# A two-layer hybrid decoder step on one core: rounding of operands moved to ScalarE, sums over values in two halves of one bank, a summed product in the state mixer, and a written-out order in the last output projection

## The chip, the cores and the metric

One Trainium2 chip, one core of it. The metric is the device time of one launch in microseconds (us). The kernel before took 1351.92 us (median of three runs, 1343.92 to 1352.94). The execution that the profiler recorded took 1348.51 us; its span, from the first to the last instruction, is 1346.5 us.

## What is computed

One inference step of two layers for a prompt of 1024 tokens and for 8 samples of 4 new tokens each, 1056 rows of 1024 features in all. Cut to what matters:

```
layer 0: h = rmsnorm(x);  xa, ga, q, k, v, gb = split(h @ w_in_ab)
         ya = RG-LRU(conv4(xa)) * silu(ga)                     # mixer A
         yb = dilated window attention(q, k, v) * silu(gb)     # mixer B, 8 heads of 64
         x  = x + concat(ya, yb) @ w_out_ab
layer 1: h = rmsnorm(x);  qc, kc, vc, gc, qd, fd, idd, gd = split(h @ w_in_cd)
         yc = rmsnorm(differential attention(qc, kc, vc)) * silu(gc)   # mixer C, 4 heads
         yd = rmsnorm(HGRN2(qd, fd, idd)) * silu(gd)                   # mixer D, 4 heads, state 128x128
         x  = x + concat(yc, yd) @ w_out_cd
y = rmsnorm(x)
sample rows attend to 256 cached keys and values (C: gathered by page table) and continue the states
```

In D a sample row's output has a part from the state that it starts with: for sample b, head j and token t it is the product of the decayed query of t with S0[b] (128x128).

## The kernel before, in words

Features lie on partitions and tokens run along the free dimension. A product that must be exact to nearly fp32 is made of rounded operands: a value is split in a high part (rounded to the replicated-fp32 type that TensorE reads in one pass) and a low part (value minus high part), and three matmuls (high by high, low by high, high by low) sum in one bank. A plain fp32 matmul shows as two records in the trace. PSUM has eight banks of 512 fp32 columns here: two for projections (`pj`), three for scores (`sc`), two for transposes (`tp`), one for sums over values (`pv`).

Six stages follow one another. The instruction names in the trace begin with the stage's letter.

- **n, a** (0 to 145 us): the norm of the input, its turn to feature rows, mixer A.
- **b** (145 to 462): mixer B, the first attention. `attention` (L1824 on) projects v, q and k for each of four pairs of heads (`qkv`), scores query blocks of 128 against keys (`scores`), and sums over values by groups of 256 queries (`groups_b`). For a group, `pv_transpose` (L701) turns the probabilities, ScalarE makes the high part PH (L704), VectorE the low part PL (L705), and L736 multiplies both by the values into one `pv` bank. At a group's end ScalarE copies the upper 64 partitions of the bank (L741) and VectorE adds the lower ones into Y (L742). VectorE rounds values (L496), queries (L520) and two copies of keys (L542, L543); GpSimd makes the low parts of keys and values (L497, L544, L545), and in this stage also those of the weights (L384).
- **o** (462 to 600): the output projection of layer 0 (`out_proj`), nine row tiles of 16 steps, each step three matmuls of 512 columns (L1201 to L1203). The attention of the sample rows (`sample_attn`) is a generator that is advanced inside these steps: transposes of cached keys (L926), logits (L936, L939), softmax (L941 to L948), the turn of the probabilities (L951, L952), products with cached values (L981, L982 cast them; L1003), a gather of the rows (L1009 to L1011).
- **d** (600 to 915): mixer D. `mixer_d` yields for each head the times from which its next step can run, `weave_d` places projection steps between. At a head's end, L1473 and L1475 add the sample part: one matmul for the new tokens, then for each of 8 samples one with S0[b] as the stationary operand and 4 columns moving. L1486 updates the states. `norm_d` follows (L1237 to L1253).
- **c** (915 to 1204): mixer C, the second attention, in the manner of b; `pv` sums at L788 and L790, copied at L794.
- **p** (1204 to 1346): the output projection of layer 1 with the sample rows of mixer C. Its cached keys and values come by indirect transfers that GpSimd issues (L1998), into five buffers in turn.

The order of work: in b, c and d a planner (`weave`, `weave_d`) writes out TensorE's order (`manual_schedule`), by clocks that it keeps for each engine with fixed costs (`spend`); `pv_free` is the planned time at which the `pv` bank is read out, and a group's first product over values isn't placed ahead of it. The other engines' order, and TensorE's in o and p, is set by the framework when the kernel is built, from its own model of times. On each engine the instructions then run in that order, each waiting for its semaphores. The framework also places all semaphore waits, from the tiles that instructions touch. `steps` in `out_proj` is the generator of the sample rows; six of each eight steps advance it by one, in the first five row tiles; what is left runs ahead of tile 5. Row tile 8 holds the sample rows and comes before the last tile.

The operands of row tile 0 of an output projection are prepared ahead, after the fifth of eight weight tiles (`finish_layer`, `operands`): the half that comes from mixer A or D at once, the other half (`rest`, with its load of `yb`) at the tile's start.

Of the kernel before, what the change touches and what calls it, by code (L numbers as in the profile page):

```python
# [8 lines left out]
F32 = mybir.dt.float32  # L9
# [40 lines left out]
def _constants():  # L50
# [19 lines left out]
    blk = blk.reshape(3 * NS, NB)  # L70
    psel = np.zeros((2, P, 4, 16), f)
    for r in range(P):
# [12 lines left out]
        "c_perm": np.ascontiguousarray(np.eye(P, dtype=f).reshape(32, 4, P)[:, ::-1].reshape(P, P)), "c_blk": blk, "c_psel": psel.reshape(2, P, 64), "c_csel": csel, "c_row": np.arange(P, dtype=np.int32)[:, None].copy(),  # L85
# [10 lines left out]
class Trunk:  # L96
# [255 lines left out]
    def to_xt(self, xn, rows, t0, pools=None):  # L352
        nc = self.nc
        for half in range(2):
            pt = self.tpsum() if pools is None or half == 0 else self.T(self.ps_s, [P, 512], F32, "sc")
# [6 lines left out]
            nc.vector.tensor_tensor(lo, src, hi.bitcast(F32), ALU.subtract)  # L362

# [35 lines left out]

    def project(self, *jobs):  # L400
        for _ in self.projection(*jobs):
            pass

    def projection(self, *jobs):
# [7 lines left out]
        for t0, n in BLKS:  # L412
            for (hi, lo), (_, _, evac) in zip(ws, jobs):
                ps = self.pj()
                xh_, xl_ = self.xt(t0, n)
                for k in range(KC):
                    xh, xl = xh_[:, k], xl_[:, k]
                    nc.tensor.matmul(ps[:, :n], hi[:, k], xh, start=(k == 0), stop=False)  # L418
                    nc.tensor.matmul(ps[:, :n], lo[:, k], xh, start=False, stop=False)  # L419
                    nc.tensor.matmul(ps[:, :n], hi[:, k], xl, start=False, stop=(k == KC - 1))  # L420
# [61 lines left out]
    def qkv(self, w, cols, outs, j, split):  # L482
# [30 lines left out]
        def split_q(a, t0, t1):  # L513
# [6 lines left out]
            nc.vector.tensor_copy(hi, src)  # L520
            nc.vector.tensor_tensor(lo, src, hi.bitcast(F32), ALU.subtract)
            self.spend("dve", 0.2 + (t1 - t0) * 1.8e-3, self.clk["act"])
# [13 lines left out]
        def split_k(a, t0, t1):  # L536
# [5 lines left out]
            nc.vector.tensor_copy(Kh[a][s, t0:t1], src)  # L542
# [3 lines left out]
            t = self.spend("dve", 0.3 + (t1 - t0) * 1.2e-3, self.clk["act"])  # L546
# [163 lines left out]

    def groups_b(self, j):

        nc, T = self.nc, self.T
        for a in range(2):
            bt = [None]
            for qc in (QLB if j == 3 and (a or QB) else QCS):
# [22 lines left out]
                def end(qc, a=a, acc=acc):  # L739
                    tmp = T(self.ap_, [64, 256], F32, "pvt")  # L740
                    nc.scalar.copy(tmp, acc[0][64:128, :256])  # L741
                    nc.vector.tensor_tensor(self.Y[64 * a:64 * a + 64, j % 2, 256 * qc:256 * qc + 256], acc[0][0:64, :256], tmp, ALU.add)  # L742
# [4 lines left out]
    def groups_c(self, h):  # L747
# [8 lines left out]
        for qc in (QLC if h == 3 else QCS):  # L756
# [27 lines left out]
            def mm(kb, p, low, q0, first, last, acc=acc):  # L784
                if first:
                    acc.append(T(self.ps_v, [P, 512], F32, "pv"))
# [6 lines left out]
            def end(qc, acc=acc):  # L793
                nc.scalar.copy(self.Y[:, h % 2, 256 * qc:256 * qc + 256], acc[0][:, :256])  # L794
# [4 lines left out]
    def weave(self, groups, after, fill, pace):  # L799
# [12 lines left out]
        more, through, prog, pv_free = True, -1, 0.0, 0.0  # L812
        inf = float("inf")
        while parts or tv:
# [12 lines left out]
            if tv and (not parts or parts[0][0] > tv[0][0]):  # L827
# [3 lines left out]
                else:  # L831
                    t_at = max(held[i, kp][1], pv_free) + LAG[2]
# [4 lines left out]
            if t_at <= max(pe, s_at):  # L837
# [12 lines left out]
                if kp == qc:  # L850
                    pv_free = end(qc)
# [12 lines left out]
    def sample_attn(self, m, load_k, load_v, is_c):  # L864
# [50 lines left out]
        for g in range(2):  # L915
            sc = T(self.ps_s, [P, 512], F32, "sc")
            for b4 in range(4):
# [4 lines left out]
                for jj in range(2):  # L922
# [6 lines left out]
                    yield  # L929
# [7 lines left out]
            yield  # L937
# [10 lines left out]
            nc.vector.tensor_scalar(pr, pr, st[:, 4:5], None, ALU.mult)  # L948
            pt = self.tpsum()
# [22 lines left out]
            yield  # L972
        psel = sc1[:, :64].rearrange("p (j c) -> p j c", j=4)
        nc.sync.dma_start(psel, self.I["c_psel"][m].rearrange("p (j c) -> p j c", j=4))
# [12 lines left out]
        for g in range(2):  # L987
            banks = [T(self.ps_s, [P, 512], F32, "sc") for _ in range(4 // per)]
# [4 lines left out]
            yield  # L993
            for b4 in range(4):
# [5 lines left out]
                for hf in range(2):  # L1000
# [4 lines left out]
                    yield  # L1005
            out = T(self.ps_v, [P, 512], F32, "pv")
            ev = T(self.wp, [P, 2, 512], F32, "wraw")
            for q, ob in enumerate(banks):
# [3 lines left out]
                yield  # L1012
# [1082 lines left out]
```

## Time and profile before

| what | value |
|---|---|
| three runs, median (lowest, highest) | 1351.92 us (1343.92, 1352.94) |
| the profiled execution: time, span | 1348.51 us, 1346.5 us |
| mean granted TensorE clock | 0.98 of 2.4 GHz |
| busy: PE, VectorE, ScalarE, GpSimd | 1289.3, 820.2, 598.2, 320.3 us |
| TensorE weight loads | 1162.3 us |
| moved by DMA | 118.9 MB, mean 88 GB/s |

PE is TensorE's matmuls, PEld its weight loads, DVE VectorE, ACT ScalarE, POOL GpSimd, SP the engine that issues most DMAs. A busy PE isn't PE at its peak: matmuls overlap, so what a stretch costs is read from the distance of starts. A bracket at the end of a timeline row says how long the engine was idle before it and what ended the wait. The granted clock is a share of 2.4 GHz; 0.5 is its lower level of 1.2 GHz. L12 is line 12 of the kernel before.

### The profile page before, as it was taken

The page shows a single profiled execution, that of the slowest core. Times are in us where ns is not written, and L with a number is a line of the kernel's source. Part 1 is how long each engine was busy: PE and PEld are TensorE (multiplying, and loading weights), DVE is VectorE, ACT ScalarE, POOL GpSimd, SP SyncE. Part 2 cuts the span into 40 slices and gives each one's busy share as a digit, 9 for nine tenths or more (in the row PEclk, how much of TensorE's full clock was granted, in tenths as well). Part 3 has the DMA queues.
Part 4 walks back from the last instruction along what each step waited for, and adds up shares of the span by engine and source line. Part 5 has one row for each costly group of instructions (what it writes and reads, how often), then busy time and mean ns, then how long its engine had stood idle before and what let it go on. Part 6 is the DMA issues. An engine that isn't in the chain of part 4 may idle for free. (4 is left out here: it accounts for less than half of the span.)

```text
span 1346.5 us, 21366 instructions
## 1 busy us (share of the span) xinstructions
PE 1289.3 (96%) x8329; PEld 1162.3 (86%) x8329; DVE 820.2 (61%) x1842; ACT 598.2 (44%) x1193; POOL 320.3 (24%) x316
## 2 busy tenths in 40 slices
PE   9999999999999889999999999999999999988997
PEld 7998999989898767879999999999898888776785
DVE  7665678787877746453646465631666566674644
ACT  7466454545455535332141414132555455563522
POOL 3456844333321300001010101012212111054300
PEclk9999999999999899999989899999999999999999
DMA  7111421312131465342111112123221223145532
GB/s 218 51 60 48 129 58 41 96 47 80 34 109 33 157 214 162 98 127 83 32 50 33 49 33 65 34 96 97 65 79 49 79 64 111 47 168 183 165 120 70
DMA packets 123674, 118.90 MB, mean 88 GB/s; under 512 B 8687, under 2 KB 104857, under 8 KB 123566
## 3 DMA queue, kind: packets, MB, share of 16 engines
q1 hardware_dynamic: 102148, 96.18, 23.1%
q10 hardware_dynamic: 18866, 12.98, 3.1%
q0 software_dynamic: 2560, 8.39, 1.9%
q8 instruction: 65, 1.06, 0.3%
q14 instruction: 35, 0.29, 0.1%
HBM read 89.20 MB, written 28.33 MB: 87 GB/s over the span
## 5 line engine op out<-in xcount | busy, mean ns | idle before, releaser
L418 PE MATMUL dpj<-oXh,dwhi 128*128 128x256 f32 (+2 forms) x384 | 134.1, 349 | 1.2 <-ACT dff L1273 1.2
L418 PE MATMUL cpj<-oXh,cwhi 128*128 128x256 f32 (+2 forms) x384 | 132.7, 346 | 0.5 <-ACT ct L593 0.5
L418 PE MATMUL bpj<-Xh,bwhi 128*128 128x256 f32 (+2 forms) x384 | 127.9, 333 | 0.4 <-ACT bt L525 0.4
L420 PE MATMUL dpj<-oXl,dwhi 128*128 128x256 f32 (+2 forms) x384 | 127.4, 332 | 0.0
L419 PE MATMUL dpj<-oXh,dwlo 128*128 128x256 f32 (+2 forms) x384 | 127.4, 332 | 0.0
L420 PE MATMUL cpj<-oXl,cwhi 128*128 128x256 f32 (+2 forms) x384 | 124.6, 324 | 0.0
L419 PE MATMUL cpj<-oXh,cwlo 128*128 128x256 f32 (+2 forms) x384 | 124.4, 324 | 0.0
L420 PE MATMUL bpj<-Xl,bwhi 128*128 128x256 f32 (+2 forms) x384 | 124.2, 324 | 0.0
L419 PE MATMUL bpj<-Xh,bwlo 128*128 128x256 f32 (+2 forms) x384 | 124.1, 323 | 0.0
L384 POOL TENSOR_TENSOR cwlo<-cwraw,cwhi 128x1024 fp32r<-128x1024 f32 x16 | 38.5, 2403 | 223.0 <-ACT cwhi L382 215.5
L418 PEld LDWEIGHTS cpj<-oXh,cwhi 128*128 128x128 f32 x384 | 72.8, 190 | 12.7 <-issue 9.2
L418 PEld LDWEIGHTS dpj<-oXh,dwhi 128*128 128x128 f32 x384 | 75.2, 196 | 3.1 <-ACT dff L1273 1.5
L419 PEld LDWEIGHTS dpj<-oXh,dwlo 128*128 128x128 f32 x384 | 75.4, 196 | 0.7
L420 PEld LDWEIGHTS dpj<-oXl,dwhi 128*128 128x128 f32 x384 | 75.2, 196 | 0.3
L418 PEld LDWEIGHTS bpj<-Xh,bwhi 128*128 128x128 f32 x384 | 72.6, 189 | 2.0 <-ACT bt L525 0.8
L635 ACT ACTIVATE bP<-bP,bsst 128x128 f32<-128x128 f32 (+3 forms) x64 | 49.6, 776 | 55.6 <-DVE bsst L632 37.9
L419 PEld LDWEIGHTS cpj<-oXh,cwlo 128*128 128x128 f32 x384 | 73.0, 190 | 1.0 <-issue 0.7
L419 PEld LDWEIGHTS bpj<-Xh,bwlo 128*128 128x128 f32 x384 | 72.8, 190 | 1.1 <-issue 0.2
L420 PEld LDWEIGHTS cpj<-oXl,cwhi 128*128 128x128 f32 x384 | 72.8, 190 | 0.3
L420 PEld LDWEIGHTS bpj<-Xl,bwhi 128*128 128x128 f32 x384 | 72.5, 189 | 0.2
L705 DVE TENSOR_TENSOR bPL<-btp,bPH 128x512 fp32r<-128x512 f32 (+1 forms) x80 | 49.2, 631 | 12.3 <-ACT bPH L704 11.6
L1201 PE MATMUL opj<-oohi,owhi 128*128 128x512 f32 x128 | 51.6, 403 | 2.1 <-ACT owhi L1149 2.1
(528 smaller groups left out, 3449.0 us busy)
## 6 DMA issues: line engine op xcount, KB each, us to landing
bwraw<-in_w_in_ab_dram SPq DMA_DIRECT2D x16, 512.0 KB
dwraw<-in_w_in_cd_dram SPq DMA_DIRECT2D x16, 512.0 KB
cwraw<-in_w_in_cd_dram SPq DMA_DIRECT2D x16, 512.0 KB
nx<-in_x_prompt_dram SPq DMA_DIRECT2D x8, 512.0 KB
bBT<-aline SPq DMA_DIRECT2D x8, 512.0 KB
owraw<-in_w_out_ab_dram SPq DMA_DIRECT2D x8, 512.0 KB
owraw<-in_cache_win_k_dram SPq DMA_DIRECT2D x8, 512.0 KB
oxres<-in_x_prompt_dram SPq DMA_DIRECT2D x8, 512.0 KB
```

The costliest lines, as they stand in the source:

```text
L384: (nc.vector if self.ph == "d" else nc.gpsimd).tensor_tensor(lo, raw, hi.bitcast(F32), ALU.subtract)
L418: nc.tensor.matmul(ps[:, :n], hi[:, k], xh, start=(k == 0), stop=False)
L419: nc.tensor.matmul(ps[:, :n], lo[:, k], xh, start=False, stop=False)
L420: nc.tensor.matmul(ps[:, :n], hi[:, k], xl, start=False, stop=(k == KC - 1))
L635: nc.scalar.activation(pr[:, :nk], pr[:, :nk], AF.Exp, bias=st[:, 2:3], accum_out=st[:, 3:4])
L705: nc.vector.tensor_tensor(pl[:, :w], pt[:, :w], ph[:, :w].bitcast(F32), ALU.subtract)
L1201: nc.tensor.matmul(ps[:rows], yh[:, kk, :rows], whi[:, c], start=(k == 0), stop=False)
```

## The change

Five things. (1) In the first attention ScalarE instead of VectorE rounds the high part of queries and of one of the two copies of keys; in both attentions it rounds the high part of values. The planner's costs follow. (2) In both attentions the sums over values use one `pv` bank that is allocated once, its two halves of 256 columns by turns, and the planner lets a group begin when the group before the last has been read out. (3) In mixer D the sample part is made in two moves: 8 matmuls with the 32 sample queries as the stationary operand and S0[b] moving (128 columns), four samples in four groups of 32 output partitions of one `sc` bank and two groups of them side by side; a copy to SBUF by ScalarE; then two matmuls with that copy as the stationary operand and a constant (`own`) of zeros and ones that picks each row's own sample. (4) The generator of the sample rows is cut in pieces in another order (keys of both groups before the first turn of probabilities) and yields how many steps to leave free; in the last output projection each of the 16 steps of a tile is a slot for it that honours these numbers, and TensorE's order there is the program's. In the output projection of layer 0 the numbers are ignored and the order stays the framework's. (5) The load of `yb` for row tile 0 is issued ahead of the split of the first half. `products` and the list that `to_xt` returns only regroup code.

```diff
@@ qkv, keep: values, both attentions
-                nc.vector.tensor_copy(hi, s[:, :, x])
+                nc.scalar.copy(hi, s[:, :, x])
                 nc.gpsimd.tensor_tensor(lo, s[:, :, x], hi.bitcast(F32), ALU.subtract)
-            t = self.spend("dve", 0.2 + 0.2 * split)
+            t = self.spend("act", 0.2 + 0.3 * split)
@@ split_q
-            nc.vector.tensor_copy(hi, src)
+            nc.scalar.copy(hi, src)
             nc.vector.tensor_tensor(lo, src, hi.bitcast(F32), ALU.subtract)
@@ split_k
-            nc.vector.tensor_copy(Kh[a][s, t0:t1], src)
+            nc.scalar.copy(Kh[a][s, t0:t1], src)
             nc.vector.tensor_copy(Kh[a][o, t0:t1], src)
@@ sums over values
+    def half_bank(self):
+        self.npv += 1
+        return self.pvb[:, 256 * (self.npv % 2):256 * (self.npv % 2) + 256]
...
-                        acc.append(T(self.ps_v, [P, 512], F32, "pv"))
+                        acc.append(self.half_bank())
...
-                    t_at = max(held[i, kp][1], pv_free) + LAG[2]
+                    t_at = max(held[i, kp][1], pv_free[0]) + LAG[2]
...
-                    pv_free = end(qc)
+                    pv_free = [pv_free[1], end(qc)]
@@ sample_attn, the new order
+        yield 10
+        yield from keys(0)
+        yield 2
+        logits(0)
+        yield 1
+        yield from keys(1)
+        yield 2
+        turned(0)
+        yield 0
+        logits(1)
+        nc.sync.dma_start(psel, self.I["c_psel"][m].rearrange("p (j c) -> p j c", j=4))
+        yield 2
+        banks = []
+        yield from values(0, banks)
+        turned(1)
+        yield 2
+        yield from ends(0, banks)
+        yield 1
+        banks = []
+        yield from values(1, banks)
+        yield 3
+        yield from ends(1, banks)
@@ operands, row tile 0
+        there = second() if i == 0 else None
         split(o, src)
...
@@ out_proj
+        def slot():
+            nonlocal hold
+            if not spaced:
+                return next(steps, None)
+            if hold:
+                hold -= 1
+            else:
+                hold = next(steps, 0)
...
-                    if k % 4 and i < 5:
-                        next(steps, None)
+                    if spaced or k % 4 and i < 5:
+                        slot()
@@ mixer_d
-        yield self.pv_free
+        yield self.scq[0]
+        ps = T(self.ps_s, [P, 512], F32, "sc")
+        for b in range(NB):
+            s0 = NS * (b % 4)
+            nc.tensor.matmul(ps[s0:s0 + NS, P * (b // 4):P * (b // 4) + P], qa[:, SEQ:NT], S0[:, b], start=True, stop=True)
+        E = T(pool, [P, 2, P], F32, "E")
+        nc.scalar.copy(E.rearrange("p r v -> p (r v)"), ps[:, :2 * P])
+        e_at = self.spend("act", 0.35, self.spend("pe", 0.55) + 0.1)
+        self.sc_done(e_at)
+        yield max(self.pv_free, e_at + 0.8)
         acc = T(self.ps_v, [P, 512], F32, "pv")
         nc.tensor.matmul(acc[:, :NS], V[:NS, 8], atS, start=True, stop=False, skip_group_check=True)
-        for b in range(NB):
-            nc.tensor.matmul(acc[:, TS * b:TS * b + TS], S0[:, b], qa[:, SEQ + TS * b:SEQ + TS * b + TS], start=False, stop=(b == NB - 1),
-                             skip_group_check=True)
+        for r in range(2):
+            nc.tensor.matmul(acc[:, :NS], E[:, r], self.own[:, r], start=False, stop=(r == 1), skip_group_check=True)
@@ finish_layer
-            self.out_proj(op, o2, ws, halves, resid, done, steps, new_xt, first)
+            if self.ph == "o":
+                return self.out_proj(op, o2, ws, halves, resid, done, steps, new_xt, first, False)
+            with self.tc.manual_schedule(engines={mybir.EngineType.PE}):
+                self.out_proj(op, o2, ws, halves, resid, done, steps, new_xt, first, True)
@@ attention
+            self.npv, self.pvb = 0, T(self.ps_v, [P, 512], F32, "pv")
@@ phase_d
+            self.own = T(self.tp_, [P, 2, NS], F32, "own")
+            nc.sync.dma_start(self.own, I["c_own"].rearrange("p (r t) -> p r t", r=2))
```

## Rows read from the trace of the kernel before

**Rows 1.** Busy time by stage: b, o, d, c, p; after the engines clock, DMA.
```profile
170.00:462.00 292.00, 276.76 (x1818) 264.31 (x1816) 232.06 (x597) 153.48 (x324) 92.05 (x74) 0.98 0.22 69
462.00:600.00 138.00, 131.23 (x682) 101.59 (x681) 73.31 (x171) 54.23 (x119) 6.42 (x20) 0.98 0.49 155
600.00:915.00 315.00, 307.66 (x2397) 295.30 (x2397) 161.62 (x283) 87.52 (x151) 32.88 (x24) 0.97 0.20 58
915.00:1204.00 289.00, 282.46 (x1848) 251.84 (x1847) 174.87 (x463) 151.48 (x316) 57.99 (x35) 0.99 0.24 73
1204.00:1346.50 142.50, 125.59 (x623) 97.30 (x621) 72.07 (x175) 52.84 (x120) 34.18 (x50) 0.96 0.46 148
```

**Rows 2.** Waits of PE, longest in total: us, times, longest.
```profile
PE bpv L736 <- DVE bY L742: 6.4, 5, 1.8
PE ptp L926 <- DMA pXh<-in_cache_k_c_dram,cidx: 4.7, 3, 2.2
PE ptp L951 <- issue: 4.6, 1, 4.6
...
PE otp L926 <- DMA owraw<-in_cache_win_k_dram: 2.9, 1, 2.9
```

**Rows 3.** Timeline of PE in d, first head, and a window behind it.
```profile
689.07 2.02 PE L1475 MATMUL dpv<-dqa,dS 128*128 128x4 f32 x16
690.94 1.20 PE L1486 MATMUL dsc<-dvx,dk 96*128 96x512 f32 x2
...
691.80:695.20 3.40, 3.40 (x14) 3.30 (x14) 3.40 (x5) 0.64 (x1) 2.64 (x2) 0.64 0.80 230
```

**Rows 4.** Chain of waits and PE timeline in p: start, us.
```profile
1247.65 1.86 PE psc L936 x30
...
1227.50 0.97 PE L939 MATMUL psc<-acs,pXh 128*128 128x32 f32 x8
```

**Rows 5.** VectorE's busy time in 140 to 465 us: L542, L520, L496.
```profile
140.00:465.00 325.00, 15.62 (x20) 0.98 0.25 77
...
140.00:465.00 325.00, 10.09 (x20) 0.98 0.25 77
...
140.00:465.00 325.00, 10.06 (x16) 0.98 0.25 77
```

**Rows 6.** One line's instructions: count, ns lowest/median/highest.
```profile
L981 ACT CAST pXl<-pXh x16: 603/622/627, 1233.3 to 1273.9; 128x512 fp32r<-128x512 f32 x16
```

**Rows 7.** Timeline in b where VectorE and GpSimd read SBUF together.
```profile
177.15 0.50 PE L624 MATMUL bsc<-bKh,bQ 128*128 128x512 f32 x1 [1.30 <-DVE bsst L627]
...
366.61 2.40 POOL L384 TENSOR_TENSOR bwlo<-bwraw,bwhi 128x1024 fp32r<-128x1024 f32 x1
366.77 2.53 DVE L542 CAST bKh<-bt 64x512 fp32r<-64x512 f32 x1
...
371.17 0.41 PE L736 MATMUL bpv<-bPH,bV 128*128 128x256 f32 x2 [0.87 <-DVE bY L742]
```

**Rows 8.** Timeline in b around the longest wait for the bank.
```profile
286.77 1.07 ACT L704 CAST bPH<-btp 128x512 fp32r<-128x512 f32 x2
...
287.40 1.28 DVE L705 TENSOR_TENSOR bPL<-btp,bPH 128x512 fp32r<-128x512 f32 x2
287.62 0.47 PE L736 MATMUL bpv<-bPH,bV 128*128 128x256 f32 x2 [1.77 <-DVE bY L742]
```

**Rows 9.** Timeline in p: VectorE reads 256 columns of a bank.
```profile
1228.51 0.43 DVE L941 CUSTOM_DVE_ANT_0 pXh<-psc,pXh 128x256 f32<-128x256 f32 x1 [3.22 <-PE psc L939]
```

**Rows 10.** Timeline in p around the longest wait, and the window behind.
```profile
1233.29 1.27 ACT L981 CAST pXl<-pXh 128x512 fp32r<-128x512 f32 x2 [8.48 <-DMA pXh<-in_cache_v_c_dram,cidx]
...
1237.25 0.66 PE L951 MATMUL ptp<-pXh 128*128 128x128 f32 x2 [4.57 <-issue]
...
1237.80:1241.20 3.40, 3.40 (x14) 2.91 (x13) 1.56 (x13) 3.02 (x12) 0.00 (x0) 0.62 0.45 121
```

**Rows 11.** Timeline of ACT in p: the eighth weight tile.
```profile
1211.22 1.05 ACT L1133 CAST pohi<-pwraw 128x1024 fp32r<-128x1024 f32 x1 [3.05 <-DMA pwraw<-in_w_out_cd_dram]
```

More of the change, by code (lines that the diff above doesn't have):

```diff
@@ L70, in _constants @@
     blk = blk.reshape(3 * NS, NB)
+    own = np.zeros((4, NS, 2, NS), f)
+    for t in range(NS):
+        own[t // 4 % 4, t, t // 16, t] = 1
     psel = np.zeros((2, P, 4, 16), f)
@@ L84, in _constants @@
         "c_flip": np.ascontiguousarray(np.eye(P, dtype=f)[::-1]),
-        "c_perm": np.ascontiguousarray(np.eye(P, dtype=f).reshape(32, 4, P)[:, ::-1].reshape(P, P)), "c_blk": blk, "c_psel": psel.reshape(2, P, 64), "c_csel": csel, "c_row": np.arange(P, dtype=np.int32)[:, None].copy(),
+        "c_perm": np.ascontiguousarray(np.eye(P, dtype=f).reshape(32, 4, P)[:, ::-1].reshape(P, P)), "c_blk": blk, "c_own": own.reshape(P, 2 * NS), "c_psel": psel.reshape(2, P, 64), "c_csel": csel, "c_row": np.arange(P, dtype=np.int32)[:, None].copy(),
     }
@@ L350, in xt, with to_xt, turn @@
         return [self.X[x, part][:, :, t0 - o:t0 - o + n] for x in "hl"]
-    def to_xt(self, xn, rows, t0, pools=None):
+    def to_xt(self, xn, rows, t0):
         nc = self.nc
-        for half in range(2):
-            pt = self.tpsum() if pools is None or half == 0 else self.T(self.ps_s, [P, 512], F32, "sc")
+        def turn(half):
+            pt = self.tpsum()
             for i in range(4):
@@ L362, in to_xt @@
             nc.vector.tensor_tensor(lo, src, hi.bitcast(F32), ALU.subtract)
+        return [lambda half=half: turn(half) for half in range(2)]
     def gain(self, pool, ap_row, tag):
@@ L398, in reset, with products @@
         self.clk = dict.fromkeys(self.clk, 0.0)
+    def products(self, ps, w, t0, n, ks):
+        nc = self.nc
+        hi, lo = w
+        xh, xl = self.xt(t0, n)
+        for k in ks:
+            nc.tensor.matmul(ps[:, :n], hi[:, k], xh[:, k], start=(k == 0), stop=False)
+            nc.tensor.matmul(ps[:, :n], lo[:, k], xh[:, k], start=False, stop=False)
+            nc.tensor.matmul(ps[:, :n], hi[:, k], xl[:, k], start=False, stop=(k == KC - 1))
     def project(self, *jobs):
@@ L412, in projection @@
         for t0, n in BLKS:
-            for (hi, lo), (_, _, evac) in zip(ws, jobs):
+            for w, (_, _, evac) in zip(ws, jobs):
                 ps = self.pj()
-                xh_, xl_ = self.xt(t0, n)
                 for k in range(KC):
[L417 to L420, printed above, removed]
+                    self.products(ps, w, t0, n, [k])
                     self.spend("pe", 3 * n / 2400)
@@ L785, in mm @@
                 if first:
[L786 removed]
+                    acc.append(self.half_bank())
                 V = self.ops[h][2]
@@ L914, in sample_attn, with keys @@
                 nc.sync.dma_start(bn[32 * b4:32 * b4 + 32, g, 4 * b:4 * b + 4], self.line_ap(m, 1020, [[LL, 8], [1, 4], [1, 4]]))
-        for g in range(2):
-            sc = T(self.ps_s, [P, 512], F32, "sc")
+        def keys(g):
             for b4 in range(4):
@@ L983, in parts, with values @@
             return hi, lo
-        for g in range(2):
-            banks = [T(self.ps_s, [P, 512], F32, "sc") for _ in range(4 // per)]
+        def values(g, banks):
+            banks.extend(T(self.ps_s, [P, 512], F32, "sc") for _ in range(4 // per))
             for n, v in enumerate(parts(self.vS)):
@@ L1004, in sample_attn, with ends @@
                                          skip_group_check=True)
-                    yield
+                    yield 0
+        def ends(g, banks):
             out = T(self.ps_v, [P, 512], F32, "pv")
@@ L1156, in operands, with second @@
         nc.sync.dma_start(src, y[:, :, t0:t0 + rows].rearrange("j p t -> p j t"))
+        def second():
+            src = space()[:, :2]
+            nc.sync.dma_start(src, self.yb[:, :, t0:t0 + rows].rearrange("j p t -> p j t"))
+            return src
+        there = second() if i == 0 else None
         split(o, src)
@@ L1161, in rest, with out_proj @@
                 return split(4 - o, self.ys)
-            src = space()[:, :2]
-            nc.sync.dma_start(src, self.yb[:, :, t0:t0 + rows].rearrange("j p t -> p j t"))
-            split(4 - o, src)
+            split(4 - o, second() if there is None else there)
             split(6 - o, self.Y[:, :, t0:t0 + rows])
         return yh, yl, rest
-    def out_proj(self, early, pool, ws, halves, resid, sink, steps, new_xt, first):
+    def out_proj(self, early, pool, ws, halves, resid, sink, steps, new_xt, first, spaced):
         nc, T = self.nc, self.T
         order = list(range(KC)) if halves[0] is not None else [4, 5, 6, 7, 0, 1, 2, 3]
+        hold = 0
+        def slot():
[6 more added lines that the diff above has]
+                hold = next(steps, 0)
         for i in (0, 1, 2, 3, 4, 5, 6, 8, 7):
@@ L1208, in out_proj @@
                     nc.vector.tensor_tensor(xr[:rows, c], rest, xr[:rows, c], ALU.add)
-            sink(i, t0, rows, xr)
+            for f in sink(i, t0, rows, xr) or []:
+                f()
     def head_norm(self, o, blocks, gcol, pool, tag):
@@ L1552, in sink0 @@
             nc.scalar.dma_start(x1d[t0:t0 + rows], x1[:rows])
-            self.to_xt(xn, rows, t0)
+            return self.to_xt(xn, rows, t0)
         with ExitStack() as st:
```

28 lines of the change are left out of this document (14 added, 14 removed).

## The prediction, made blind

> **What bounds the kernel now.** I read the busy times by stage first, then TensorE's waits, then the timeline around each of them. TensorE is busy for 1289 of 1346.5 us, and in no stage is another engine near it: in the first attention VectorE has 232 of 292 us and ScalarE 153 [rows 1]. So little can be had beyond two things: TensorE's idle time (15.2 us in the first attention b, 6.8 in the output projection o, 7.3 in mixer D, 6.5 in the second attention c, 16.9 in the last projection p, part of that the tail after the last matmul) [rows 1], and stretches in which its clock is at the lower level. The largest waits are those for the bank of sums over values in b (6.4 us in five), for gathered keys in p (4.7 in three), and one of 4.6 us in p ahead of the turn of the sample rows' probabilities [rows 2]. The reader is to see that the idle time is spread thin, so that no single edit can bring more than one or two per cent.
>
> **Mixer D.** The sample part is now 16 records that move 4 columns each, in 1.87 us from the first to the start of what follows [rows 3]. Behind it the granted clock is 0.64 in a window of 3.4 us, that is partly 1.2 GHz: (1 - 0.64) x 3.4 = 1.2 us of work lost there, and with the beginning of the fall I take 1.5. There are four such windows, one behind this block of each head; one stands in [rows 3]. The change puts in 16 records of 128 columns in four column groups and 4 records of 32 columns. The nearest row for the first is 30 records of 256 columns, also in four groups, in 1.86 us, 0.062 each; half the columns cost between half of that and all of it, 0.5 to 1.0 us. The second costs as L939 does, 0.97 / 8 = 0.12 each, 0.5 [rows 4]. So 1.0 to 1.5 us in place of 1.87: 0.4 to 0.9 saved, four times 1.6 to 3.6; I take 2.4. The clock: the new block comes in two pieces with projection between, and the longer one moves wide operands, so I count three of the four falls as gone, 4.5 us. Together **7 us**. Bounds: 10 (all falls gone, best price) and a loss of 2 (ScalarE's copy between the pieces, 0.5 us at each head, is waited for, and the falls stay). The constant's load and the copy itself are hidden: ScalarE has 88 of 315 us there [rows 1].
>
> **First attention, rounding.** VectorE loses 15.6 (keys), 10.1 (queries) and 10.1 us (values) [rows 5]. ScalarE gains 56 casts: the nearest row is 0.62 us for 512 columns [rows 6]; as many of these are narrower, I take 0.5, 28 us in all, against its 153 of 292. VectorE's mean for a key copy is 15.62 / 20 = 0.78 us, but one took 2.53 us, from 366.77, in the same time as a GpSimd subtraction of 2.40 from 366.61 [rows 7]. The VectorE work behind such a copy is what TensorE then waits for: 0.87 us at 371.17 and 1.30 at 177.15 [rows 7]; a third of this kind is about as long as the first. These three go, 3.1 us, and I add 1 us for smaller ones: **4 us**. The Trainium skill, in "SBUF — State Buffer", section Who interferes with whom, says that VectorE and GpSimd share a pair of ports that one of them locks for a whole instruction, and that ScalarE never waits on anyone; the pair of rows at 366 agrees with the first half, and no row here shows the second. By that rule the moved casts keep their 0.5 us; were they stretched as VectorE's was, to 2.5, the 16 late ones would put 32 us into ScalarE's queue and the term would be a loss.
>
> Bounds of this term. Upwards: all of 15.2 us, and four falls of the clock in b and at its end at 1.5, 21. Downwards: queued behind ScalarE's new casts are its high parts of probabilities (L704) and the copy of the bank (L741). Sixteen casts (two operands, two halves, four pairs of heads) are placed late, amid the scores; if each stands ahead of a high part that TensorE waits for, 16 x 0.62 = 10 us are lost.
>
> **Bank halves.** TensorE's longest wait for the bank ended at 287.62; the high parts that it needs next were made in 286.77 to 287.84, two in 1.07, so the first at about 287.3, and the low parts from 287.40 to 288.68 [rows 8]. Freed from the bank it would have waited for those, so even a bank with free halves gives 0.3 us there and hardly 1.5 in the five waits. And the halves are likely not free: VectorE's read of 256 columns of a score bank at 1228.51 waited for L939, which writes other columns of that bank [rows 9]; waits go by bank. I take **0**. The Trainium skill, in "PSUM — Partial Sum Buffer", section PSUM bank collisions raise a hardware error, says that two engines must not be in the same bank on the same quadrant at once, whichever columns they touch; by it the second half can't be filled while the first is read, as the row at 1228.51 has it, and this edit brings nothing. Without rule and row it would be 1.5. The planner's earlier release changes little: a group's first product comes after its own transposes and their high and low parts, which end later than the copy and the sum of the bank. At 287.4 that order is to be seen [rows 8].
>
> **Second attention.** Its value casts move too; ScalarE has 151 of 289 us and VectorE 175, and TensorE's idle time is 6.5 [rows 1]. **0**, between -3 and 3, as plans shift.
>
> **Last projection.** The wait of 4.57 us at 1237.25 is for the softmax, which VectorE and ScalarE had queued behind the cast of gathered values (ScalarE idle for 8.48 us until they landed); behind it the clock is 0.62 for 3.4 us, 1.3 us lost [rows 10]. In the new order the turn of one group's probabilities stands behind the keys of the next, and value loads are first needed far later; this wait and fall go, 5.9 us. Of the 4.7 us for gathered keys [rows 2], ten free steps at the start take the first two waits away, but TensorE then reaches the eighth weight tile, whose cast ScalarE began at 1211.22 after 3.05 us of waiting for its DMA [rows 11]; it stops there as long. I count 0.8 for the third. Now that TensorE's order is fixed, three waits are new: each bank is copied by ScalarE right ahead of its gather (twice), and the norm of the sample rows comes soon behind the last gather; 0.6 us each by the cast [rows 6], 1.7. **5 us.** On the queues: SP's `psel` load moves behind the logits, POOL's gathers keep their order, and the free buffers limit them as before. Upper bound: 4.7 + 4.6 + two falls, 12; the lower is the slow rival's.
>
> **Projection of layer 0.** `yb` arrives earlier for tile 0, but TensorE's first wait there is for a cached-key load (2.9 us) [rows 2], which stays. The new order of pieces helps as in p, though less was lost: **1 us**, between -3 and 4, since the framework reorders TensorE here by its own model.
>
> **Sum.** 7 + 4 + 0 + 0 + 5 + 1 = 17. Against the profiled execution, 1348.5 - 17 = 1331.5; the median of the runs shown is 3.4 us above that execution, which would give 1335. I say **1333**.
>
> **Rivals.** (1) The clock falls in D as before and the waits in p only change places: D gives 2.4, p 2, the rest 5, about 9: 1341. For it: falls of the clock elsewhere follow shorter pauses, such as that at 287.6. Against: the block with 4 columns is gone. (2) VectorE's relief clears the first attention: 15 instead of 4: 1322. For it: most waits of b end with VectorE [rows 2]; against: the longest has ScalarE's high parts just ahead of it [rows 8]. (3) **Slower**: in p, 18 casts of values (L981, 0.62 us [rows 6], and VectorE's low part, 1.28 / 2 [rows 8]) stand right ahead of their products in TensorE's fixed order. If each pair is bare, 18 x 1.26 = 23 us; with the waits that go (6.7), p loses 16, against 12 gained elsewhere: 1355. It decides once a step's bare wait is above 1.0 us on average. Against it: `units` holds five buffers of 512 columns, which lets casts run two steps ahead. (4) ScalarE becomes late in b: the loss of 10 and two falls, 13 in place of the gain of 4: 1350.
>
> **Chances.** Forecast 0.52 (own range 1324 to 1340), rival 1 0.20, rival 2 0.12, rival 3 0.09, rival 4 0.07. A measurement of this kernel tells about 1% (13.5 us) from no change. Faster by over 1%, under 1338: rival 2 and 0.48 of the forecast, 0.60. Slower by over 1%, above 1365: only the far ends of rivals 3 and 4, 0.05. Within: 0.35. The range of 8 in 10 takes in rival 2 and rival 1 and most of rival 4's neighbourhood: 1318 to 1348.
>
> **What would show it.** Right: in D, one `sc` copy per head, no block of 4-column records, clock at 1.0 behind it; in b, no VectorE cast at L520 or L542 lines and shorter waits for low parts, while waits of L736 for Y go on; in p, no wait of 4 us ahead of the turn of probabilities. Wrong: TensorE waiting in p ahead of products with cached values, high parts in b coming late behind ScalarE's casts, or falls of the clock that only move.

## The result, and the profile after

The changed kernel takes 1327.41 us (median of four runs, 1326.29 to 1330.77), the kernel before 1348.45 in the same comparison (1343.92 to 1352.94): ratio 0.986, 95% interval 0.9827 to 0.9892. A second comparison, on another occasion, gave 1332.07 against 1345.66, 0.9891 (0.9857 to 0.9924). So the gain is 14 to 21 us; the forecast was 17, 1333 us. The profiled execution has a span of 1326.1 us against 1346.5.

To set stages side by side, both kernels are cut at the first product of each stage's projection (b, o, d, c, p; the last stage ends with the span). These are not the bounds of [rows 1], so the rows of before stand here too. Columns: stretch, length, busy time and count of TensorE, its weight loads, VectorE, ScalarE, GpSimd; granted clock, share of the DMA engines, GB/s. Before:

```profile
135.40:461.70 326.30, 310.61 (x2030) 297.65 (x2029) 253.21 (x620) 168.63 (x346) 119.36 (x96) 0.98 0.24 75
461.70:603.60 141.90, 135.13 (x704) 104.54 (x703) 75.12 (x174) 54.74 (x121) 6.67 (x20) 0.98 0.49 155
603.60:905.00 301.40, 294.06 (x2314) 282.58 (x2313) 158.94 (x278) 84.70 (x145) 29.34 (x21) 0.97 0.18 52
905.00:1206.30 301.30, 293.12 (x1914) 262.14 (x1912) 178.35 (x468) 156.07 (x322) 63.52 (x39) 0.99 0.25 79
1206.30:1346.50 140.20, 124.93 (x620) 96.97 (x619) 69.77 (x172) 50.55 (x118) 32.19 (x49) 0.96 0.45 145
```

After:

```profile
135.30:453.60 318.30, 307.30 (x2030) 296.61 (x2029) 218.18 (x565) 192.75 (x403) 120.54 (x96) 0.98 0.25 78
453.60:593.50 139.90, 136.22 (x705) 104.63 (x704) 74.45 (x173) 54.76 (x121) 6.08 (x20) 0.98 0.48 154
593.50:887.50 294.00, 283.88 (x2329) 270.80 (x2328) 162.51 (x278) 86.14 (x149) 31.05 (x21) 0.99 0.19 53
887.50:1187.40 299.90, 292.04 (x1915) 261.00 (x1913) 170.32 (x458) 159.35 (x329) 64.34 (x38) 1.00 0.25 78
1187.40:1326.10 138.70, 122.69 (x621) 94.88 (x620) 72.19 (x174) 55.54 (x121) 34.83 (x50) 0.97 0.48 150
```

The first attention gained 8.0 us, layer 0's projection 2.0, mixer D 7.4, the second attention 1.4, the last stage 1.5, in this pair of profiles. The reader should split each difference in two. Length less busy time is TensorE's **idle time**: in b it fell from 15.7 to 11.0, in D it rose from 7.3 to 10.1. What is left is **busy time**. The instructions are nearly the same in number, so it moves mostly with the clock, in D also with the new block: there it fell by 10.2.

TensorE's waits after, the longest in total (us, times, longest); they answer to [rows 2]:

```profile
PE ppj L1269 <- DVE pwlo L1198: 5.8, 2, 4.9
PE dsc L1315 <- DVE dhlo L1305: 5.5, 4, 1.7
PE bpv L753 <- ACT bPH L716: 4.8, 7, 1.3
PE bpv L753 <- DVE bPL L717: 3.6, 9, 1.5
...
PE bpv L753 <- DVE bY L759: 1.1, 1, 1.1
```

The waits for the bank of sums (6.4 us in five before), for gathered keys and ahead of the turn are gone or small. Two are new at the top: one at the start of the last projection, and one for the low part of the squares in D's norm.

### The profile page after: what moved, and what is told of

Same layout as the page of the kernel before. It is cut to its first block, busy times and chain, and to the rows that moved or that the text cites. A ratio compares the mean times of both kernels' runs of the same rounds, so it can differ in the third digit from the quotient of the medians.

```text
span 1326.1 us, 21393 instructions
## 1 busy us (share of the span) xinstructions
PE 1274.2 (96%) x8345; PEld 1147.1 (87%) x8345; DVE 782.5 (59%) x1778; ACT 632.0 (48%) x1263; POOL 326.0 (25%) x316
## 5 line engine op out<-in xcount | busy, mean ns | idle before, releaser
L412 PE MATMUL dpj<-oXh,dwhi 128*128 128x256 f32 (+2 forms) x384 | 131.2, 342 | 1.7 <-ACT dff L1340 1.2
L414 PE MATMUL dpj<-oXl,dwhi 128*128 128x256 f32 (+2 forms) x384 | 124.7, 325 | 0.0
L413 PE MATMUL dpj<-oXh,dwlo 128*128 128x256 f32 (+2 forms) x384 | 124.3, 324 | 0.0
L412 PEld LDWEIGHTS cpj<-oXh,cwhi 128*128 128x128 f32 x384 | 72.5, 189 | 15.5 <-issue 8.1
L1269 PE MATMUL ppj<-pohi,pwlo 128*128 128x512 f32 x128 | 51.1, 399 | 5.8 <-DVE pwlo L1198 5.8
```

The costliest lines, as they stand in the source:

```text
L412: nc.tensor.matmul(ps[:, :n], hi[:, k], xh[:, k], start=(k == 0), stop=False)
L413: nc.tensor.matmul(ps[:, :n], lo[:, k], xh[:, k], start=False, stop=False)
L414: nc.tensor.matmul(ps[:, :n], hi[:, k], xl[:, k], start=False, stop=(k == KC - 1))
L1269: nc.tensor.matmul(ps[:rows], yl[:, kk, :rows], whi[:, c], start=False, stop=(k == KC - 1))
```

## Experiments

The code changes are shown shortened. A ratio is known to about 0.003 either way, and several intervals below overlap those of the changed kernel; so what an edit did is read from its stage, from idle time above all.

**What repeats and what does not.** Both kernels ran again without an edit. On the changed kernel:

> The changed kernel once more, without an edit: what of the stage times comes back, and what does not. Theory (TensorE's idle time belongs to the program, the places of the clock's falls do not): idle time of 11 to 12 us in the first attention, 10.1 in mixer D, 15.5 to 16.5 from the first product of the last projection to the end, as in the first profile; falls of the clock at other places, so that a stage differs by 1.7 us for each of them and the whole by up to 6 us. Rival (the falls belong to the program too): falls at the same places within a few us, and every stage within 1 us of the first profile.

1332.07 us, ratio 0.9891 (0.9857 to 0.9924). Idle times 11.0 us in b and 10.1 in D, as in the first profile, and 17.5 in p against 16.0, outside the expected 15.5 to 16.5. Falls of the clock elsewhere: in D one at 750 us became one at 689 and a double one at 811, each in or right behind one of the three waits of 1.7 us for the norm's low part. D took 297.1 us with three falls and 294.0 with one: idle time the same, busy time 3.1 more. A fall costs about 1.7 us by the rows around the first one in the kernel before (granted clock 0.83 and 0.67 in two windows of 3.4 us: (0.17 + 0.33) x 3.4). Idle time belongs to the program in b, D and the second attention (within 0.2 us), less so in the two output projections, where it moved by 1.8 and 1.5 us; most falls belong to the run. A comparison of two profiles alone can be wrong by several us.

> The kernel before once more, without an edit. TensorE's idle time by stage should come back within 0.5 us (first attention 15.7, mixer D 7.3, last stage 15.3), as that of the changed kernel did. Theory (the unbroken narrow block starts falls of the clock): three to six falls in mixer D again, at least three of them right behind a block, TensorE busy there for 289 to 294 us. Rival (six were chance): two or fewer, busy for 286 us or less.

Ratio 1.000 (0.9964 to 1.0035). Idle 16.0, 7.3 and 14.2 us in b, D and p, the last beyond the expected half microsecond. Mixer D showed five falls, three right behind the block of a head, two some 10 us further, where the first profile has them too; busy for 292.7 us. Here the falls do belong to the program. The block of the first head, a stretch of 3.4 us in which the clock drops, and one in the second fall of that head:

```profile
683.84 1.95 PE L1475 MATMUL dpv<-dqa,dS 128*128 128x4 f32 x16
...
684.40:687.80 3.40, 3.40 (x19) 3.21 (x19) 1.52 (x4) 1.28 (x2) 0.84 (x1) 0.70 0.15 36
694.60:698.00 3.40, 3.27 (x13) 3.17 (x14) 0.08 (x1) 3.02 (x4) 0.94 (x1) 0.71 0.00 0
```

TensorE is busy throughout the first stretch, and its timeline shows no wait from 660 us on: this fall follows no pause, only a row of products that move 4 columns. In the two profiles of before and the next run, 10 of 12 such blocks have a fall behind them.

**Mixer D: the block put back, cut up, and cut up in the kernel before.** In the changed kernel the sample part became the old one again:

```
-  16 records of 128 columns into a score bank; ScalarE copies it to E; 4 records of own x E
+  for b in range(NB): matmul(acc[:, 4b:4b+4], S0[:, b], qa[4 columns of b])   # one piece
```

> The changed kernel with mixer D's sample part as it was: eight products of 4 columns (16 records) in one piece, nothing else altered. Lengths are from the first matmul of a stage to the first of the next; the changed kernel has 294.0 us in mixer D, the kernel before 301.4. Theory (the block and the falls of the clock behind it make the difference): mixer D takes 300 to 302 us, a window with a granted clock under 0.8 is back behind at least three of the four blocks, and the run takes about 7 us more than the changed kernel's 1327.4, about 1334.5. Rival (the falls only move, and the difference comes from another place of the schedule): mixer D takes 294 to 297 us, the run 1327 to 1330.

1330.78 us, ratio 0.9888 (0.9857 to 0.9919). D took 295.4 us, so by length the rival has it. But the sum hides two opposite terms. Mixer D in the run with the block put back, then the changed kernel's second run:

```profile
594.70:890.10 295.40, 289.42 (x2314) 278.35 (x2314) 157.28 (x278) 84.59 (x145) 29.63 (x21) 0.98 0.18 53
```
```profile
593.40:890.50 297.10, 286.96 (x2329) 273.52 (x2328) 163.20 (x278) 86.11 (x149) 30.02 (x21) 0.98 0.18 53
```

With the old block TensorE is idle for 6.0 us, with the new one for 10.1. Busy time is 5.5 us above the first profile of the changed kernel (three falls, each behind a block, against one). The new block itself brought a wait. Next, the old products in pairs:

```
+  if b in (2, 4, 6): yield clk["pe"] + 0.6     # products of a projection go between the pairs
```

> The changed kernel with the old eight products of 4 columns in mixer D, but in four pairs with products of a projection between them: the old work without the old unbroken stretch of narrow operands. Theory (two causes: the work costs 1.87 against about 1.1 us a head, the falls about 1.2 us a head): no fall of the clock below 0.8 behind the pairs; mixer D takes 294.0 + 4 x 0.8 = 297 us, between the changed kernel's 294.0 and the kernel with the whole block at about 301. Rival 1 (the work is everything, the clock nothing): as with the whole block, 300 to 302 us. Rival 2 (the clock is everything): 294 to 295 us.

1325.66 us, ratio 0.9858 (0.9831 to 0.9886). D took 291.2 us, busy for 285.7, idle for 5.5, no stretch under 1.0: shorter than the changed kernel, which nobody expected. The second row is the new block without a fall, from a run below in which D is as in the changed kernel (the last projection's order put back):

```profile
595.80:887.00 291.20, 285.69 (x2314) 273.65 (x2313) 152.89 (x278) 83.46 (x145) 32.14 (x21) 1.00 0.19 54
```
```profile
591.70:884.50 292.80, 282.67 (x2330) 269.65 (x2329) 161.72 (x278) 86.22 (x149) 32.07 (x21) 1.00 0.19 54
```

So the old work in pairs is 3.0 us dearer than the new in busy time, but it sets off neither a fall nor the new wait. The same edit in the kernel before:

> The kernel before with one edit: mixer D's eight products of 4 columns in four pairs with products of a projection between them. Before: mixer D 301.4 us, TensorE busy for 294.1 of them, idle for 7.3, clock at 0.97. Theory (the unbroken narrow block starts the falls of the clock, and these are the larger part of what the change gained in mixer D): at most two falls are left in mixer D, TensorE is busy for 285 to 288 us, mixer D takes 291 to 295 us, and the ratio to the kernel before is 0.993 to 0.996. Rival (the falls come at random or from the waits ahead of the norm, 5.4 us in seven): mixer D takes 299 us or more, the ratio is above 0.997.

Ratio 0.9962 (0.9938 to 0.9986). Mixer D before a second time, then with its block cut:

```profile
598.30:898.30 300.00, 292.67 (x2314) 281.21 (x2314) 159.02 (x278) 84.64 (x145) 29.30 (x21) 0.97 0.18 52
```
```profile
600.20:893.00 292.80, 285.60 (x2314) 273.58 (x2313) 158.09 (x278) 83.61 (x145) 31.66 (x21) 1.00 0.19 54
```

The same 2314 records, the same idle time (7.3 and 7.2 us), and 7.1 us less busy: that is the clock (five falls at 1.7 us would be 8.5). This was as much as the whole edit of D brought in the first pair of profiles. The second falls, 10 us behind the block, went as well, though the waits near them stayed; why is open.

**The new wait in D's norm.** In the changed kernel (first head; start, duration, engine, line, out and operands, idle time before and its releaser):

```profile
677.54 0.64 PE L1543 MATMUL dsc<-dS,dqa 128*32 128x128 f32 x16
678.25 0.37 ACT L1545 COPY dE<-dsc 128x256 f32<-128x256 f32 x1
680.76 0.63 PE L1553 MATMUL dpv<-down,dE 128*128 128x32 f32 x4
...
687.23 2.03 POOL L1536 TENSOR_TENSOR dS<-dS,dtt 128x1024 f32<-128x1024 f32 x1
687.61 2.10 DVE L1305 TENSOR_TENSOR dhlo<-dhsq,dhhi 128x416 fp32r<-128x416 f32 x1
689.76 0.46 PE L1315 MATMUL dsc<-dhlo,nones 128*128 128x416 f32 x1 [1.74 <-DVE dhlo L1305]
...
681.20:684.60 3.40, 3.40 (x21) 3.31 (x21) 2.85 (x5) 1.29 (x2) 1.89 (x1) 1.00 0.31 88
```

The new block works as announced: 0.64 us, 0.47 from the first of the four products to what follows at 681.23, and a clock of 1.0 behind it. But the subtraction for the third block of squares now falls beside GpSimd's product: 2.10 us. In the run with the old block put back the same shape took 0.58, when GpSimd's product had ended:

```profile
687.88 1.90 POOL L1536 TENSOR_TENSOR dS<-dS,dtt 128x1024 f32<-128x1024 f32 x1 [2.19 <-DMA out_s_d_s_dram<-dS]
690.40 0.58 DVE L1305 TENSOR_TENSOR dhlo<-dhsq,dhhi 128x416 fp32r<-128x416 f32 x1
```

By the Trainium skill ("SBUF — State Buffer", Who interferes with whom) a VectorE instruction with two operands in SBUF contends with a GpSimd instruction that reads there, and the one issued later blocks. The trace agrees: the subtraction began 0.38 us behind the product and ended 0.45 us behind the product's end, not far from the 0.58 that it takes alone. So ScalarE was given this rounding as well:

```
-  nc.vector.tensor_copy(hi, v)        # norm_d, split
+  nc.scalar.copy(hi, v)
```

> The changed kernel with one more high part moved: the squares of mixer D's norm are rounded by ScalarE instead of VectorE (12 casts; the third of a head now stands right ahead of the products that wait for it, 0.8 us for the high part and 1.7 for the low part behind it, in three heads). Theory (VectorE's cast and subtraction are late because the cast is made by VectorE beside GpSimd's products; ScalarE makes it in about 0.55 us): TensorE's idle time in mixer D falls from 10.1 to 5 to 7 us, mixer D takes 289.5 to 292 us instead of 294.0, the run about 1324. Rival (the low part still meets GpSimd's product and is stretched as before, or ScalarE is late with the logarithms): idle for 9 us or more, mixer D 293 to 295 us.

1322.13 us, ratio 0.9822 (0.9786 to 0.9858); mixer D:

```profile
597.20:884.40 287.20, 282.61 (x2329) 269.55 (x2328) 151.44 (x266) 90.86 (x161) 32.35 (x21) 1.00 0.19 55
```

Idle time of 4.6 us and the length are even below the expectation; no wait for the low part is over 0.4 us, there is no fall, and the stage takes 6.8 us less than in the changed kernel. Two more profiles with this edit (below) have 287.2 and 287.3.

**Rounding.**

```
-  nc.scalar.copy(hi, ...)             # values, queries, first copy of keys
+  nc.vector.tensor_copy(hi, ...)      # and the planner's costs of before
```

> The changed kernel with the high parts of values, queries and the first copy of keys made by VectorE again, with the planner's costs of before; bank halves and everything else stay as changed. The first attention has 318.3 us in the changed kernel and 326.3 in the kernel before. Theory (VectorE's relief is what the first attention gained): it takes 325 to 327 us here, the run about 1335; waits of TensorE for low parts grow, and windows with a low clock come back. Rival (the planner's freer bank of sums is what it gained): it takes 318 to 320 us, the run 1327 to 1329.

1335.7 us, ratio 0.9938 (0.9915 to 0.9961). The first attention took 324.7 us, just short of the 325 expected, and was idle for 16.0, as before; waits for low parts did not grow (3.0 us, 3.6 in the changed kernel). The stage and its waits:

```profile
134.70:459.40 324.70, 308.74 (x2030) 296.22 (x2029) 254.77 (x622) 168.78 (x347) 119.38 (x96) 0.98 0.24 76
```
```profile
PE bpv L753 <- DVE bY L759: 6.5, 5, 1.8
PE bpv L753 <- DVE bPL L717: 3.0, 7, 1.5
PE bpv L753 <- ACT bPH L716: 2.2, 5, 0.7
```

The five waits for the bank are back, though the sums still go to halves by turns in this kernel: the one that ends at 286.89 is for the addition of the group just before (286.33 to 286.74), which reads the other half. They come from VectorE's lateness, or from the order that the planner makes by its costs; the two were put back in one edit.

> The changed kernel with only the first copy of keys made by VectorE again (20 casts, 15.6 us of VectorE in the kernel before, some of them beside a GpSimd subtraction and then up to 2.53 us long); queries and values stay with ScalarE. With all three back the first attention took 324.7 us, against 318.3. Theory (the stretched key casts are the larger part of what was gained): 321.5 to 324 us, TensorE idle for 13 to 15 us there. Rival (queries and values carry the gain, by their number): 318 to 320.5 us, idle for 11 to 12.5.

1335.3 us, ratio 0.9915 (0.9881 to 0.9949). The length, 324.9 us, is outside both expectations, because of falls (clock 0.97); idle time is 13.9 us, as the theory had it: the keys, with their cost in the planner, hold 2.9 of the 5.0 us.

```profile
135.60:460.50 324.90, 310.97 (x2031) 299.04 (x2030) 232.34 (x584) 183.11 (x383) 119.70 (x95) 0.97 0.24 76
```

The casts of the first copy of keys, in this kernel and in the changed one (count, ns lowest/median/highest):

```profile
L554 DVE CAST bKh<-bt x20: 277/357/2530, 165.4 to 365.5; 64x384 fp32r<-64x384 f32 x8, 64x512 fp32r<-64x512 f32 x8, 64x256 fp32r<-64x256 f32 x4
```
```profile
L554 ACT CAST bKh<-bt x20: 406/513/618, 163.2 to 358.3; 64x384 fp32r<-64x384 f32 x8, 64x512 fp32r<-64x512 f32 x8, 64x256 fp32r<-64x256 f32 x4
```

ScalarE is slower at the median and never stretched.

**Bank halves.**

```
-  acc = pvb[:, 256 * (npv % 2):][:, :256];  pv_free = [pv_free[1], end(qc)]
+  acc = T(ps_v, [P, 512], F32, "pv")[:, :256];  pv_free = end(qc)
```

> The changed kernel with a bank of its own again for every group's sums over values in both attentions (one buffer, as before), and the planner holding a group back until the last sum is copied; rounding stays on ScalarE. The first attention has 318.3 us in the changed kernel, the second 299.9. Theory (a bank is held as a whole, so halves by turns free nothing): the first attention takes 318 to 320 us, the second 299 to 301, TensorE's idle time in the first stays at 10.5 to 12.5 us (11.0 in the changed kernel). Rival (the other half can be filled while the first is read, and the planner uses it): the first attention takes 323 us or more, with waits for the bank of over 4 us in all back.

1331.12 us, ratio 0.9903 (0.9868 to 0.9938); its interval overlaps both of the changed kernel. First attention 316.8 us, idle for 11.07, second 300.1; the waits, row for row those of the changed kernel:

```profile
PE bpv L753 <- ACT bPH L716: 4.9, 7, 1.3
PE bpv L753 <- DVE bPL L717: 3.7, 9, 1.5
PE bpv L753 <- DVE bY L759: 1.1, 1, 1.1
```

Here the edit brings nothing; the single remaining wait for the bank stands in both kernels.

**The last projection.** The order of the sample part and TensorE's own order put back for p alone:

> The changed kernel with the last projection's sample part in its former order and without the spaced fixed order of TensorE there; the projection of layer 0 stays as changed. The last stage has 138.7 us in the changed kernel and 142.0 in the kernel before, to the end of the run. Theory (the order took away the waits of 4.6 us ahead of the turned probabilities and part of those for gathered keys): 142 us here, the run about 1331; the wait of 4 us and more ahead of the turn is back. Rival (the gain came from the end of the run or of the tail, not from the order): 138 to 140 us, the run 1327 to 1329.

1332.88 us, ratio 0.9924 (0.9895 to 0.9952). From its first product to the end p took 141.3 us, against 138.7 (before: 140.2 by the same bound; the 142.0 of the expectation counted from the end of the projection ahead). Its waits, and the stage:

```profile
PE ptp L972 <- issue: 5.2, 1, 5.2
PE ptp L943 <- DMA pXh<-in_cache_k_c_dram,cidx: 4.1, 3, 2.9
```
```profile
1184.80:1326.10 141.30, 125.41 (x620) 97.63 (x619) 71.36 (x174) 51.33 (x119) 35.05 (x49) 0.95 0.46 146
```

So the order takes both waits away, 9.3 us, yet TensorE's idle time in p is no less for it: 15.9 us here, 16.0 and 17.5 in the two profiles of the changed kernel, which waits at the start instead. The 2.6 us of length are busy time, and one pair can't show them: with p as in the changed kernel, eight profiles have 136.6 to 141.0 us (mean 138.8), with p as before three have 140.2 to 142.6 (mean 141.2). At the start the chain is, in the changed kernel:

```profile
1190.95 0.41 ACT L1197 CAST pwhi<-pyin 128x256 fp32r<-128x256 f32 x1
1194.37 1.04 ACT L1181 CAST pohi<-pwraw 128x1024 fp32r<-128x1024 f32 x1 [3.01 <-issue]
1195.44 1.23 DVE L1182 TENSOR_TENSOR polo<-pwraw,pohi 128x1024 fp32r<-128x1024 f32 x1 [2.45 <-ACT pohi L1181]
1196.59 0.42 DVE L1198 TENSOR_TENSOR pwlo<-pyin,pwhi 128x256 fp32r<-128x256 f32 x1
1197.06 0.80 PE L1269 MATMUL ppj<-pohi,pwlo 128*128 128x512 f32 x1 [4.92 <-DVE pwlo L1198]
```

The operand's high part is ready at 1191.36; its low part stands in VectorE's queue behind the eighth weight's, which waits for ScalarE's cast of that weight. What the cast waits for this profile doesn't name (`issue`); in the changed kernel's second profile it is the weight's load, and cast and products both wait 1.6 us longer:

```profile
1200.25 1.04 ACT L1181 CAST pohi<-pwraw 128x1024 fp32r<-128x1024 f32 x1 [4.61 <-DMA pwraw<-in_w_out_cd_dram]
...
1202.95 0.80 PE L1269 MATMUL ppj<-pohi,pwlo 128*128 128x512 f32 x1 [6.52 <-DVE pwlo L1198]
```

The next kernel, with D's norm on ScalarE, splits the rest of tile 0 ahead of that weight:

```
+  if k == 6 and not new_xt: first[2]()     # the rest of tile 0's operands
```

> ScalarE rounds the squares of mixer D's norm (as in the run before, 1322.1 us), and in the last projection the rest of tile 0's operands is split ahead of the eighth weight tile, not behind it. There TensorE waited 4.9 to 5.7 us for a low part that stood in VectorE's queue behind the low part of that weight (which waits for ScalarE's cast, and that for the load). Theory (the queue is the cause): TensorE takes up the products 0 to 2 of the second half while the weight loads, the wait falls to 2.5 to 4 us and now ends with the eighth weight; the last stage takes 136.5 to 138 us instead of 138.7, the run about 1320.5. Rival (the eighth weight itself sets the time, and the first rest is hidden behind it anyway): the wait stays at 4.5 us or more, the stage at 138 to 139.5 us, the run at 1322.

**1321.37 us**, ratio 0.9818 (0.9785 to 0.9851), the fastest here, though not to be told from 1322.13. The wait for L1198 fell to 2.2 us in two, the longer 1.3 where it had been 4.9: the queue was its cause. The stage took 137.6 us, as expected, but that is within what p takes without the edit:

```profile
PE ptp L943 <- ACT pwhi L1197: 2.5, 1, 2.5
PE ppj L1269 <- DVE pwlo L1198: 2.2, 2, 1.3
...
PE ppj L1268 <- DVE polo L1182: 0.8, 1, 0.8
```

Part of it came back as 2.5 us ahead of the first turn of keys, behind a later operand's cast.

> As the kernel with the rest of tile 0 split ahead of the eighth weight, and with 6 free places instead of 10 ahead of the first turn of gathered keys, so that these turns stand in TensorE's order where it waits for the weight. Theory (the keys have landed by then): the wait at the start falls by another 1 to 2 us, the last stage takes 135 to 137 us, the run about 1319. Rival (the gathered keys land later than the weight, and the fixed order makes TensorE wait for them instead): waits for gathered keys of 2 us or more are back, the stage takes 138 to 141 us.

1325.37 us, ratio 0.9852 (0.982 to 0.9884). The rival: 2.3 us for gathered keys are back, the stage took 141.3 us, and all six runs (1325.01 to 1328.69) lie above the six with ten free places (1318.12 to 1323.96). Of the two numbers ten is the better.

## Why the prediction was right, and where its steps were not

The total came out as forecast; the terms did so less neatly. By the first pair of profiles D brought 7.4 (7 said), b 8.0 (4), c 1.4 (0), p 1.5 (5) and o 2.0 (1). By the second pair they brought 2.9, 2.2, 0.2, -0.1 and 2.8. The means over all profiles here in which a stage is untouched (six to eleven with the change, two or three without) are firmer: D 5.8, b 5.2, c 1.4, p 2.5, o 1.6, together 16.5. That errors of both signs add up to the 17 is luck.

**D, 7.** The work was sized about right: 0.64 + 0.47 = 1.1 us a head in place of 1.87, 3.0 in all (2.4 said), which is also the difference in busy time between pairs and new block, both without a fall. The falls were mis-sized: six and five in two profiles of before, at about 1.7 us, not four at 1.5, since those some 10 us behind a block were not counted; cutting the block alone gave 7.1 us back. And a loss was missed: the step costed ScalarE's copy, which nothing waits for, but not what is late next, the norm's low part, 2.8 us more idle time. Two misses of opposite sign made the sum fit. Rival 1, that falls only move, holds in part: those behind the block are gone, but with the new block all seven stretches of low clock in D, in six profiles, begin in one of the three waits of 1.7 us or less than 1 us behind it. They went when the wait went. Outside D many falls move from run to run.

**b, 4.** Idle time fell by 4.7 us (15.7 and 16.0 before, 11.0 in both profiles after): that is the term. The other 3.3 of the first pair are busy time and vary: with the same first attention, b took 315.6 to 322.6 us in the kernels above. The reason was half right. Stretched key casts cost 2.9 us, about as said. But the text expected waits for Y to go on: they went, from 6.4 to 1.1 us, since VectorE's sum came earlier, and waits for ScalarE's high parts grew from 1.9 to 4.8; those for low parts, which were to get shorter, went from 2.8 us in six to 3.6 in nine. At the place of [rows 8] TensorE now waits 1.30 us for the high part where it had waited 1.77 for the bank: 0.5 us less, near the "0.3 us there". ScalarE's casts did not make it late enough for rival 4. The Trainium skill ("SBUF — State Buffer", Who interferes with whom) says of ScalarE that it never waits on anyone: the trace agrees, none of 20 casts over 0.618 us.

**Bank halves, 0.** Right, and for the reason given: with halves and the old rounding the waits for the bank stay, 6.5 us in five. This shows how the program waits; whether the bank itself would allow more was not tried.

**c, 0**, came at 1.4 within its bounds (0.2 by the second pair); which edit brought it is open.

**p, 5.** Both waits went, and the stop at the start came, as written; it was 4.9 us in one profile and 6.5 in the other, not about 4. The step that failed is the size of that stop: it was put down to the eighth weight, but it ends with an operand queued behind that weight on VectorE. Idle time in p did not fall at all (15.3 and 14.2 before, 16.0 and 17.5 after): the stop cost what the two waits had cost. What p gained is busy time, 2.5 us by the means, and its cause is not shown. Rival 3, bare value casts, did not come: the longest wait ahead of a value product was 0.8 us.

**o, 1.** 1.6 by the means; the wait for a cached key, which the text thought would stay, fell from 2.9 to 0.7 us in the first pair of profiles and from 2.7 to 1.9 in the second. No run isolates it.

## What to carry to other kernels

Compare two profiles by idle time and by busy time: in the changed kernel the first repeated within half a microsecond in three stages of five, the second carries falls of the clock that differ from run to run. A shorter block moves everything behind it, so ask which operand now meets another engine; here that cost 2.8 us until one more cast was moved. An operation queued in order behind one that waits for a load is as late as the load, whatever its own inputs do.

## What the hardware showed unexpectedly

The clock fell to its lower level with TensorE busy, behind 16 products of 4 columns in one piece (granted clock 0.70 over 3.4 us), in 10 of 12 such blocks; the same products in four pairs, with wide products between, left it at 1.00 throughout mixer D, in both kernels that had them. A VectorE subtraction of 128x416 took 2.10 us beside a GpSimd product of 2.03 that began 0.38 us earlier, and 0.58 us where that product had ended.
